# A hybrid state-space block on one core: the first two units of the feed-forward product in turn, and the time-step product of B11 made once

## The chip, the core and the metric

The kernel runs on one core of one Trainium2 chip. The core has five engines with a queue of instructions each: TensorE (PE, matrix products into PSUM banks), VectorE (DVE), ScalarE (ACT), GpSimd (POOL) and SyncE (SP, which here only issues transfers). Each engine takes its instructions strictly in the order of the program's text; an instruction that reads another engine's result waits on a semaphore, and everything behind it on its engine waits with it. The metric is the device time of one execution in microseconds (us), the median of several.

## The reference, cut to what matters

One layer over x (1024 tokens x 1024 features, float32):

```python
h = x + hybrid_mixer(rmsnorm(x, norm_mix_w), w_in, ...)
h = h + swiglu(rmsnorm(h, norm_ffn_w), w_gate, w_up, w_down)
return rmsnorm(h, final_norm_w)

# in hybrid_mixer
u = h @ w_in                               # 1024 x IN_DIM
z, xbc, dt_raw, s_b, s_c, s_x, g_a, g_b = split(u)
dt = softplus(dt_raw + dt_bias)            # 1024 tokens x 32 heads: the "time steps"
...                                        # conv, chunked state-space scan, gated norm, second mixer, w_o

def swiglu(h, w_gate, w_up, w_down):
    return (silu(h @ w_gate) * (h @ w_up)) @ w_down      # hidden size 2816
```

Two places of it are touched: `dt_raw`, which is the normed x times 32 columns of w_in, and the product of the normed h with w_gate and w_up.

## The kernel before, in words

**Products.** The engine's fp32r type holds fewer bits than float32, so every float32 operand is split in two parts of that type: ACT copies the operand (the high part, names ending in h: wh, th), DVE subtracts that copy from the operand (the low part: wl, tl), and three matmuls, high x high (L679), low x high (L680) and high x low (L681), are added up in PSUM. Splitting is `split` (ACT at L76, DVE at L77); one 128x1024 page takes one instruction on each.

**Seven products instead of eight.** Large products are done in a two by two block scheme. Of the turned, normed input, B11 and B21 are the two halves of the features of the first 512 tokens. The second 512 tokens give B12 and B22; of these the kernel keeps B22 and the sums T1 = B12 - B11, T2, T3 and T4 = B21 - T2 with the signs of the scheme. On the weights' side there are A11, A12, A22 and the sums S1 to S4. Product n (1 to 7) multiplies one of each: 1: B11, 2: B21, 3: B22, 4: T4, 5: T1, 6: T2, 7: T3. They run in the order 1, 2, 6, 5, 7, 3, 4.

**The start of the kernel.** Rows of x are loaded, their squares summed (`rows_sq`, ACT at L117 and DVE at L115), scaled (`rows_scale`, L137), turned by PE against the identity (`turn_rows`, L1542, into banks pt), copied out with the norm weight (`turned_out`, ACT at L1549 and DVE at L1551, into br) and split by `put` into th and tl. Then come the first three `Pair`s p0, p1, p2: column blocks of w_in for z, each with a high part (`hi`, ACT at L864), a low part (`lo`, DVE at L868), its matmuls (`pe`, into banks pb and pd) and the copying out (`ev`, ACT at L890). They run product by product: product 1 of p0, p1 and p2, then product 2 of all three, and so on; T1 to T4 are made in between. The text runs: split B11; p0 product 1; `wdt_split` (L1512, splits the 32 columns of w_in for the time steps); `steps_pe(0, 0)`; squares of rows 4 to 7 (L117, L115); p1 high and low part; p1 product 1; squares; copy p0 out (L890); p2 high and low part; p2 product 1; copying out of B21's rows; split B21; scaling of rows 4 to 7; and so on.

**The time steps.** `steps_pe(hf, part)` multiplies the 128x32 weight tiles by the first (hf 0) or second (hf 1) half of the tokens into a bank ts. hf 0 takes B11 (12 matmuls, part 0) and B21 (12, part 1). hf 1 needs B12, which is not kept, and takes B11 and then T1 for it (24 matmuls, part 0), and B22 (12, part 1). Both parts of hf 1 stand just ahead of the first product that uses T3. `time_steps` (at about 113 us) copies both banks out with the bias (L299, ACT, 32x512 each) and does the rest of the softplus and the sums.

**The feed-forward product.** `ffn_phase` (L1163) works on units of 128 columns of w_gate and 128 of w_up for each half of the hidden size. A unit has seven steps, one for each product: split the weights (`prep`, L1241), 24 matmuls (`pe`), copy or add the banks out (`ev`, L1261 and on). Step s = 7u + k is product number k in the order above of unit u. `load_to(n)` issues the weight loads of the first n pages: SP loads a page (L1237), and for S1 to S4 POOL adds a second operand onto it by a transfer that accumulates (L1236, L1239). In text order the steps run 0, 1, 7, 8, 2, 3, 4, 5, 6, 9, 10, ...: products 1 and 2 of the first two units, then what is left of unit 0, then of unit 1. The sums T2, T1, T3, B22 and T4 of this stage are made by a generator, `second_half` (L1191; T4's adds at L1211), which is advanced by one piece behind certain steps. Product n = 7 reads T3, 3 reads B22, 4 reads T4; and steps 4, 5 and 6 are these three of unit 0.

Of the kernel before, what the change touches and what calls it, by code (L numbers as in the profile page):

```python
# [8 lines left out]
F32 = mybir.dt.float32  # L9
F32R = mybir.dt.float32r  # L10
AF = mybir.ActivationFunctionType
ALU = mybir.AluOpType

P = 128
# [6 lines left out]
H = G * HPG  # L21
# [18 lines left out]
def hybrid_block(ctx: ExitStack, tc: tile.TileContext, x, nmw, w_in, cw, cb, dtb, alog, dsk, snw,  # L40
                 wssd, scw, wsc, wo, nfw, wg, wu, wd, fnw, out):
    nc = tc.nc
# [7 lines left out]
    sp = ctx.enter_context(tc.tile_pool(name="sp", bufs=2))  # L50
# [9 lines left out]
    def page(s, shape=(P, 1024), dt=F32):  # L60
        return pp.tile(list(shape), dt, tag="pg", name=nm(s))

    def bank(s):
        return sm.tile([P, 512], F32, tag="sm", name=nm(s))
# [156 lines left out]
    def every(gen):  # L221
        for _ in gen:
            pass
# [24 lines left out]
    dtbc = cp.tile([H, 1], F32, name="dtbc")  # L248
# [38 lines left out]
    pac = cp.tile([P, NT, H], F32, name="pac")  # L287
    V = nc.vector

    def time_steps(ps):  # L290

        a = cp.tile([P, 1], F32, name="a")
        nc.scalar.activation(a, al, AF.Exp)
        V.tensor_scalar_mul(a, a, -1.0)
        t1, t2 = page("ts", (P, 4, 256)), page("ts", (P, 4, 256))
        u, e, r, q, ac = t1[:, 0], t1[:, 1], t1[:, 2], t1[:, 3], t2[:, 0]
        raw = page("tr", (H, S))
        for hf in range(2):
            nc.scalar.activation(raw[:, hf * 512:hf * 512 + 512], ps[hf][:H], AF.Identity, bias=dtbc)  # L299
        for i in range(4):  # L300
            nc.sync.dma_start(u[32 * i:32 * i + 32, :], raw[:, i * 256:i * 256 + 256])
        nc.gpsimd.memset(ac, 1.0)
        nc.gpsimd.memset(ac.rearrange("h (c l) -> h c l", l=P)[:, :, 0:1], 0.0)

        def rest():
            yield
            yield
            yield
            V.scalar_tensor_tensor(e, u, -1.0, u, op0=ALU.mult, op1=ALU.max)
            nc.scalar.activation(e, e, AF.Exp, scale=-1.0)  # L310
            yield
            V.tensor_scalar_add(r, e, 2.0)
            V.reciprocal(r, r)
            yield
            V.tensor_mul(e, e, r)
            V.tensor_mul(q, e, e)
            V.tensor_scalar_mul(r, q, 2.0 / 17)
            yield
            for n in (15, 13, 11, 9, 7, 5, 3):
                V.scalar_tensor_tensor(r, r, 2.0 / n, q, op0=ALU.add, op1=ALU.mult)  # L320
                if n in (11, 5):
                    yield
            V.scalar_tensor_tensor(r, r, 2.0, e, op0=ALU.add, op1=ALU.mult)
            V.scalar_tensor_tensor(u, u, 0.0, r, op0=ALU.max, op1=ALU.add)
            yield
            V.tensor_scalar_mul(e, u, a)
            V.tensor_tensor_scan(q, ac, e, 0.0, op0=ALU.mult, op1=ALU.add)
            yield

            def keep(d, t):  # L330
                for i in range(4):
                    nc.sync.dma_start(d[2 * i:2 * i + 2].rearrange("c h l -> h c l"),
                                      t[32 * i:32 * i + 32, :].rearrange("h (c l) -> h c l", l=P))
            keep(ac_d, q)
            q3 = q.rearrange("h (c l) -> h c l", l=P)
            r3 = r.rearrange("h (c l) -> h c l", l=P)
            V.tensor_sub(r3, q3[:, :, P - 1:P].to_broadcast([P, 2, P]), q3)
            yield
            nc.scalar.activation(r, r, AF.Exp)
            nc.scalar.activation(e, q, AF.Exp)  # L340
            keep(e_d, e)
            yield
            V.tensor_mul(r, r, u)
            yield
            for src, dst in ((u, dtt), (q, pac), (r, wdt)):
                pt = bank("tt")
                for c in range(2):
                    nc.tensor.transpose(pt[:, c * P:(c + 1) * P], src[:, c * P:(c + 1) * P], ident)
                for c in range(2):
                    nc.scalar.activation(dst.rearrange("p (q c) h -> p c q h", c=2)[:, c],  # L350
                                         pt[:, c * P:(c + 1) * P].rearrange("p (q h) -> p q h", h=H), AF.Copy)
            yield
        side.append(rest())
# [324 lines left out]
    def mmc(o, lh, ll, rh, rl, first, last):  # L678
        nc.tensor.matmul(o, lh, rh, start=first, stop=False, skip_group_check=True)  # L679
        nc.tensor.matmul(o, lh, rl, start=False, stop=False, skip_group_check=True)  # L680
        nc.tensor.matmul(o, ll, rh, start=False, stop=last, skip_group_check=True)  # L681
# [147 lines left out]
    def half_b(name, k):  # L829
        h, l = T[name][k // 2]  # L830
        return h[:, k % 2, :], l[:, k % 2, :]
# [331 lines left out]
    def ffn_phase():  # L1163
# [152 lines left out]
        steps = [s for st, _ in units for s in st]  # L1316
# [3 lines left out]
        def load_to(n):  # L1320
            while done[0] < min(n, len(loads)):
                u, f = loads[done[0]]
                units[u][1](f)
                done[0] += 1


        def early_weights():
            load_to(3)
            yield
            load_to(4)  # L1330
            steps[0][0]()
            yield
            steps[1][0]()
            load_to(5)
            yield
            load_to(6)
            yield
            steps[2][0]()
            load_to(8)
            yield  # L1340
            steps[7][0]()
            load_to(9)
            yield

        weights, rows = early_weights(), first_half()
# [10 lines left out]
        gen = second_half(rows1)  # L1356
        steps[0][1]()
        steps[0][2]()
        steps[8][0]()
        steps[3][0]()  # L1360
        steps[1][1]()
        for _ in range(4):
            next(gen, None)
        steps[1][2]()
        for _ in range(4):
            next(gen, None)
        steps[7][1]()
        steps[7][2]()
        next(gen, None)
        steps[8][1]()  # L1370
        next(gen, None)
        steps[8][2]()
        for s in range(2, 6):
            steps[s][1]()
            steps[s][2]()
            next(gen, None)
            if s < 5:
                steps[s + 2][0]()
                load_to(s + 8)
        every(gen)  # L1380

        sq = cp.tile([P, NT, 2], F32, name="sqf")
# [61 lines left out]
                yield  # L1444

        ds = Stream(Gemm(FU, fa_d, fb_d, ORDER, NEG_B, ev_d))
        rest = steps[6:7] + steps[9:]
        rest[1][0]()
        for i, (_, pe, ev) in enumerate(rest):
            load_to(14 + i)  # L1450
            while later and next(later[0], 0) == 0:
                later.pop(0)
            if i >= len(rest) - 4:
                ds.ahead(i - len(rest) + 5, i - len(rest) + 2)
            pe()
            ev()
            if i + 2 < len(rest):
                rest[i + 2][0]()
# [45 lines left out]
    small_loads()  # L1504
    loaded[0] = NF
    steps_ps, wdt_hl = [], []

    def wdt_split():
        for d in range(2):
            t = sp.tile([P, 512], F32R, tag="st", name=nm("wdt"))  # L1510
            wdt_hl.append(t[:, 0:KT * H].rearrange("p (k h) -> p k h", h=H))
        nc.scalar.activation(wdt_hl[0], wdt_s, AF.Copy)  # L1512
        V.tensor_sub(wdt_hl[1], wdt_s, wdt_hl[0].bitcast(F32))

    def steps_pe(hf, part):

        wh, wl = wdt_hl
        if part == 0:
            steps_ps.append(bank("ts"))
        names = ((("B11",), ("B21",)), (("B11", "T1"), ("B22",)))[hf][part]  # L1520
        todo = [(n, k) for n in names for k in range(4)]
        for j, (n, k) in enumerate(todo):
            bh, bl = half_b(n, k)
            kw = 4 * part + k
            mmc(steps_ps[hf][:H], wh[:, kw, :], wl[:, kw, :], bh, bl, j == 0 and part == 0,
                j == len(todo) - 1 and part == 1)

    a0 = rows_sq(xt[0:4], "x", "avav")
    a1 = rows_acc(xt[4:8], "x")
# [95 lines left out]
    gen = second_half()  # L1625
# [25 lines left out]
    for i in range(7 * NF, n_slots):  # L1651
        slot(i)
        if i == 7 * NF + 4:
            time_steps(steps_ps)
            del steps_ps[:]
        if i == 7 * NF + 14:
            d_skip_columns()
        make(i)
        load_pairs((i + 11) // 7 + 1)
        pump()  # L1660
        if i % 3 == 0:
            next(sums, None)
        if i % 3 == 1:
            pump_aux()
        left = n_slots - 1 - i
        if left in (4, 3, 2):
            del T[{4: "T2", 3: "T1", 2: "T3"}[left]]
        if left == 9:
            b12 = [page("br", HB) for _ in range(2)]
            for k in range(2):  # L1670
                nc.sync.dma_start(b12[k], b12_d[k])
        if left == 7:
            direct[0][0].load()
        if left == 4:
            every(put("B12", b12))
        if left == 3:
            direct_hi(direct[0][0])
            direct[1][0].load()
        if left == 2:
            direct_lo(direct[0][0])  # L1680
            pump_scan()
# [42 lines left out]
```

## Time and profile before

| | us |
|---|---|
| median of 3 executions | 1930.08 (1929.77 to 1930.65) |
| profiled execution, its own time | 1931.04 |
| span of its trace (first to last instruction) | 1929.3 |
| PE busy in the span | 1887.9 (98%) |
| DVE busy | 1291.1 (67%) |
| ACT busy | 965.0 (50%) |
| POOL busy | 181.4 (9%) |
| mean granted TensorE clock | 0.995 |

A row of a timeline gives the start in us from the span's beginning, the time to the end of the last of its instructions, the engine, the line, the operation, output<-inputs, partitions x elements, and how many like instructions are drawn together (x1, x2); in square brackets stands how long the engine was idle just ahead of it and what released it. A row of the waits gives the waiting group, what ended the wait, the time waited in total, how many times, and the longest. A row of the windows gives the stretch, its length, and per engine the busy time with the number of instructions; then the granted TensorE clock (1.00 is full speed), the DMA engines' busy share and GB/s.

### The profile page before, as it was taken

The page shows a single profiled execution, that of the slowest core. Times are in us where ns is not written, and L with a number is a line of the kernel's source. Part 1 is how long each engine was busy: PE and PEld are TensorE (multiplying, and loading weights), DVE is VectorE, ACT ScalarE, POOL GpSimd, SP SyncE. Part 2 cuts the span into 40 slices and gives each one's busy share as a digit, 9 for nine tenths or more (in the row PEclk, how much of TensorE's full clock was granted, in tenths as well). Part 3 has the DMA queues.
Part 4 walks back from the last instruction along what each step waited for, and adds up shares of the span by engine and source line. Part 5 has one row for each costly group of instructions (what it writes and reads, how often), then busy time and mean ns, then how long its engine had stood idle before and what let it go on. Part 6 is the DMA issues. An engine that isn't in the chain of part 4 may idle for free.

```text
span 1929.3 us, 24107 instructions
## 1 busy us (share of the span) xinstructions
PE 1887.9 (98%) x8917; PEld 1550.9 (80%) x8917; DVE 1291.1 (67%) x1660; ACT 965.0 (50%) x1533; POOL 181.4 (9%) x168
## 2 busy tenths in 40 slices
PE   7999999999999999999989999999999999999998
PEld 5688888888887888888868888887888888888886
DVE  7667878677774868887878548877444444456465
ACT  5545454444446877777546454465333333345333
POOL 1010111010100101010100000101221121100000
PEclk9999999999999999999989999999999999999999
DMA  5297999988959557768669766736998788867562
GB/s 179 62 260 170 242 233 232 229 207 227 272 138 289 189 180 252 246 220 275 209 243 373 233 222 203 207 125 133 227 205 208 199 192 200 217 259 287 193 196 109
DMA packets 345094, 411.97 MB, mean 214 GB/s; under 512 B 17192, under 2 KB 223744, under 8 KB 344976
## 3 DMA queue, kind: packets, MB, share of 16 engines
q1 hardware_dynamic: 293232, 325.39, 51.7%
q0 software_dynamic: 43680, 55.67, 18.2%
q10 hardware_dynamic: 8064, 29.36, 3.8%
q8 instruction: 70, 1.15, 0.2%
q14 instruction: 48, 0.39, 0.1%
HBM read 320.56 MB, written 143.15 MB: 240 GB/s over the span
## 4 chain that ended last, share of the span: by engine, by line
PE 87%; DVE 6%; ACT 3%; DMA 2%; issue 1%; SPq 0%; ACTq 0%; DVEq 0%
PE pb L679 5%; PE pb L680 5%; PE pb L681 5%; PE gb L680 5%; PE gb L679 5%; PE gb L681 5%; PE fb L681 4%; PE fb L679 4%; PE fb L680 4%; PE pr L81 4%; PE pr L83 4%; PE gd L679 4%; PE gd L680 4%; PE gd L681 4%; PE pr L82 4%; PE pd L679 4%
## 5 line engine op out<-in xcount | busy, mean ns | idle before, releaser
L77 DVE TENSOR_TENSOR wl<-ws,wh 128x1024 fp32r<-128x1024 f32 x77 | 94.0, 1222 | 121.5 <-ACT wh L76 121.5
L680 PE MATMUL gb<-ql,gh 128*128 128x512 f32 x432 | 169.7, 393 | 3.2 <-DVE ql L77 3.2
L679 PE MATMUL gb<-qh,gh 128*128 128x512 f32 x432 | 169.6, 393 | 1.1 <-DVE h L1132 1.1
L681 PE MATMUL gb<-qh,gl 128*128 128x512 f32 x432 | 169.3, 392 | 0.0
L81 PE MATMUL pr<-th,wh 128*128 128x512 f32 x352 | 144.2, 410 | 0.0
L83 PE MATMUL pr<-th,wl 128*128 128x512 f32 x352 | 138.2, 393 | 2.0 <-DVE wl L990 2.0
L681 PE MATMUL fb<-th,wl 128*128 128x512 f32 x352 | 137.2, 390 | 0.8 <-DVE wl L77 0.8
L679 PE MATMUL fb<-th,wh 128*128 128x512 f32 x352 | 137.3, 390 | 0.6 <-ACT wh L76 0.6
L82 PE MATMUL pr<-tl,wh 128*128 128x512 f32 x352 | 137.5, 391 | 0.0
L680 PE MATMUL fb<-tl,wh 128*128 128x512 f32 x352 | 137.1, 390 | 0.0
L679 PE MATMUL gd<-qh,gh 128*128 128x512 f32 x324 | 127.0, 392 | 0.0
L680 PE MATMUL gd<-ql,gh 128*128 128x512 f32 x324 | 126.7, 391 | 0.0
L681 PE MATMUL gd<-qh,gl 128*128 128x512 f32 x324 | 126.7, 391 | 0.0
L77 DVE TENSOR_TENSOR ql<-cb,qh 128x1024 fp32r<-128x1024 f32 x98 | 118.0, 1204 | 2.6 <-ACT qh L76 2.5
L76 ACT ACTIVATE qh<-cb 128x1024 fp32r<-128x1024 f32 x98 | 99.9, 1019 | 38.4 <-PE gb L680 17.2
L679 PE MATMUL fd<-th,wh 128*128 128x512 f32 x264 | 102.8, 390 | 0.0
L681 PE MATMUL fd<-th,wl 128*128 128x512 f32 x264 | 102.8, 390 | 0.0
L680 PE MATMUL fd<-tl,wh 128*128 128x512 f32 x264 | 102.8, 389 | 0.0
L74 DVE SCALAR_TENSOR_TENSOR gl<-ca,gh 128x1024 fp32r<-128x1024 f32 (+1 forms) x60 | 72.8, 1214 | 44.4 <-ACT gh L73 44.4
L680 PEld LDWEIGHTS gb<-ql,gh 128*128 128x128 f32 x432 | 81.8, 189 | 20.7 <-DVE ql L77 3.9
L679 PEld LDWEIGHTS gb<-qh,gh 128*128 128x128 f32 x432 | 81.8, 189 | 18.7 <-DVE h L1132 1.4
L681 PEld LDWEIGHTS gb<-qh,gl 128*128 128x128 f32 x432 | 81.9, 189 | 16.9
(319 smaller groups left out, 4681.7 us busy)
## 6 DMA issues: line engine op xcount, KB each, us to landing
ws<-in_w_in_dram SPq DMA_DIRECT2D x80, 512.0 KB, 7.1
ws<-in_w_gate_dram SPq DMA_DIRECT2D x77, 256.0 KB, 3.9
ws<-in_w_up_dram SPq DMA_DIRECT2D x77, 256.0 KB, 4.4
ca<-u_d SPq DMA_DIRECT2D x35, 512.0 KB, 5.5
ab<-ac_d SPq DMA_DIRECT2D x32, 512.0 KB, 6.9
xbc_g<-cv ACTq DMA_DIRECT2D x24, 512.0 KB, 7.0
ws<-ws POOLq DMA_DIRECT2D x22, 512.0 KB, 6.5
wd_d<-in_w_down_dram SPq DMA_DIRECT2D x20, 512.0 KB, 9.8
```

The source lines that it names most:

```text
L74: nc.vector.scalar_tensor_tensor(lo, src, -1.0, hi.bitcast(F32), op0=ALU.mult, op1=ALU.subtract)
L76: nc.scalar.activation(hi, src, AF.Copy)
L77: nc.vector.tensor_sub(lo, src, hi.bitcast(F32))
L81: nc.tensor.matmul(o, lh, rh, start=first, stop=False)
L82: nc.tensor.matmul(o, lh, rl, start=False, stop=False)
L83: nc.tensor.matmul(o, ll, rh, start=False, stop=last)
L679: nc.tensor.matmul(o, lh, rh, start=first, stop=False, skip_group_check=True)
L680: nc.tensor.matmul(o, lh, rl, start=False, stop=False, skip_group_check=True)
L681: nc.tensor.matmul(o, ll, rh, start=False, stop=last, skip_group_check=True)
```

## The change

Two parts that share nothing but the kernel.

**Time steps.** The 12 matmuls of B11 for the second half of the tokens are dropped. In their place the bank of the first half, which after `steps_pe(0, 0)` holds just B11's part, is copied out with the bias by one ACT instruction (32x512, into a new tile dt11) as soon as that part is done. The second half's bank gets T1 and B22 only, and `time_steps` adds dt11 to it on DVE instead of copying it on ACT.

**Feed-forward product.** After steps 0, 1, 7 and 8 the steps run 2, 9, 3, 10, 4, 11, 5, 6, 12, 13, 14, ...: products 6, 5 and 7 of units 0 and 1 in turn, then 3 and 4 of unit 0 and 3 and 4 of unit 1. The generator of the sums is advanced behind every second of these steps. The weights are loaded ahead in the order of the pages as before, up to page 11 instead of 9 by the early part and further ahead after it; the splitting of step 9's weights now stands behind the eighth piece of the generator, and that of step 3's weights, which stood ahead of step 1's matmuls, now follows step 2.

```diff
@@ time_steps
-    def time_steps(ps):
+    def time_steps(ps, dt11):
...
-        for hf in range(2):
-            nc.scalar.activation(raw[:, hf * 512:hf * 512 + 512], ps[hf][:H], AF.Identity, bias=dtbc)
+        nc.scalar.activation(raw[:, 0:512], ps[0][:H], AF.Identity, bias=dtbc)
+        V.tensor_add(raw[:, 512:1024], dt11, ps[1][:H])
@@ ffn_phase, early_weights
             steps[7][0]()
-            load_to(9)
+            load_to(11)
@@ ffn_phase, the first units
         steps[8][0]()
-        steps[3][0]()
+        seq = [2, 9, 3, 10, 4, 11, 5, 6, 12, 13] + list(range(14, len(steps)))
         steps[1][1]()
         for _ in range(4):
             next(gen, None)
         steps[1][2]()
         for _ in range(4):
             next(gen, None)
+        steps[9][0]()
         steps[7][1]()
         steps[7][2]()
         next(gen, None)
         steps[8][1]()
         next(gen, None)
         steps[8][2]()
-        for s in range(2, 6):
-            steps[s][1]()
-            steps[s][2]()
-            next(gen, None)
-            if s < 5:
-                steps[s + 2][0]()
-                load_to(s + 8)
+        for j in range(6):
+            load_to(12 + j)
+            steps[seq[j]][1]()
+            steps[seq[j]][2]()
+            if j % 2:
+                next(gen, None)
+            steps[seq[j + 2]][0]()
         every(gen)
...
-        rest = steps[6:7] + steps[9:]
-        rest[1][0]()
+        rest = [steps[i] for i in seq[6:]]
         for i, (_, pe, ev) in enumerate(rest):
-            load_to(14 + i)
+            load_to(18 + i)
@@ the start
+    dt11 = sp.tile([P, 512], F32, tag="eb", name="dt11")[:H, :]
...
     def steps_pe(hf, part):
         wh, wl = wdt_hl
         if part == 0:
             steps_ps.append(bank("ts"))
-        names = ((("B11",), ("B21",)), (("B11", "T1"), ("B22",)))[hf][part]
-        todo = [(n, k) for n in names for k in range(4)]
-        for j, (n, k) in enumerate(todo):
-            bh, bl = half_b(n, k)
+        ps = steps_ps[hf][:H]
+        name = (("B11", "B21"), ("T1", "B22"))[hf][part]
+        for k in range(4):
+            bh, bl = half_b(name, k)
             kw = 4 * part + k
-            mmc(steps_ps[hf][:H], wh[:, kw, :], wl[:, kw, :], bh, bl, j == 0 and part == 0,
-                j == len(todo) - 1 and part == 1)
+            mmc(ps, wh[:, kw, :], wl[:, kw, :], bh, bl, k == 0 and part == 0, k == 3)
+        if (hf, part) == (0, 0):
+            nc.scalar.activation(dt11, ps, AF.Identity, bias=dtbc)
@@ second half of the mixer
-            time_steps(steps_ps)
+            time_steps(steps_ps, dt11)
```

What this does to the order of ACT's instructions at the start, where th is B11's high part, wdt the time-step weights, xn the rows whose squares are summed, wh the high part of p1's and then p2's weights, u p0's result and br B21's turned rows. Before:

```order
L76 ACTIVATE th_284<-br_254 128x1024
L76 ACTIVATE th_288<-br_260 128x1024
L1512 ACTIVATE wdt_305<-wdts 128x256
L117 ACTIVATE xn_324,xss_215<-x_90 128x1024
L864 ACTIVATE wh_326<-ws_189 128x1024
L117 ACTIVATE xn_345,xss_215<-x_92 128x1024
L890 ACTIVATE u_347<-pb_292 128x512
L864 ACTIVATE wh_349<-ws_191 128x1024
L1549 ACTIVATE br_366<-pt_264,cols 128x512
```

With the change, the same stretch:

```order
L76 ACTIVATE th_285<-br_255 128x1024
L76 ACTIVATE th_289<-br_261 128x1024
L1513 ACTIVATE wdt_306<-wdts 128x256
L1529 ACTIVATE dt_206<-ts_310,dtbc 32x512
L117 ACTIVATE xn_326,xss_216<-x_90 128x1024
L864 ACTIVATE wh_328<-ws_189 128x1024
L117 ACTIVATE xn_347,xss_216<-x_92 128x1024
L890 ACTIVATE u_349<-pb_293 128x512
L864 ACTIVATE wh_351<-ws_191 128x1024
L1552 ACTIVATE br_368<-pt_265,cols 128x512
```

The copy into dt11, which reads the bank ts, now stands ahead of everything that ACT does for the squares and for the weights of p1 and p2; nothing else of this stretch has moved.

On DVE, around the making of T4 in the feed-forward product (br is T4, made in place from B21 by L1211 and split into tl; L1284 and L1259 are the `ev` of a product 7, L1289 the start of that of a product 3, wl the low part of weights). Before:

```order
L77 TENSOR_TENSOR tl_10896<-br_10718,th_10895 128x1024
L77 TENSOR_TENSOR wl_10900<-ws_10269,wh_10899 128x1024
L1284 TENSOR_TENSOR c_10888<-c_10888,fb_10610 128x512
L1284 TENSOR_TENSOR c_10888<-c_10888,fb_10611 128x512
L1259 TENSOR_TENSOR ub_10700<-c_10888 128x512
L1211 TENSOR_TENSOR br_10516<-br_10516,t_1727_10764 128x1024
L1211 TENSOR_TENSOR br_10529<-br_10529,t_1728_10765 128x1024
L77 TENSOR_TENSOR tl_10938<-br_10516,th_10937 128x1024
L77 TENSOR_TENSOR tl_10942<-br_10529,th_10941 128x1024
L77 TENSOR_TENSOR wl_10946<-ws_10315,wh_10945 128x1024
L1289 TENSOR_TENSOR c_10840<-c_10840,fd_10862 128x512
```

With the change:

```order
L77 TENSOR_TENSOR wl_11008<-ws_10259,wh_11007 128x1024
L1284 TENSOR_TENSOR c_10961<-c_10961,fb_10730 128x512
L1284 TENSOR_TENSOR c_10961<-c_10961,fb_10731 128x512
L1259 TENSOR_TENSOR ub_10810<-c_10961 128x512
L1211 TENSOR_TENSOR br_10515<-br_10515,t_1729_10763 128x1024
L1211 TENSOR_TENSOR br_10528<-br_10528,t_1730_10764 128x1024
L77 TENSOR_TENSOR tl_11047<-br_10515,th_11046 128x1024
L77 TENSOR_TENSOR tl_11051<-br_10528,th_11050 128x1024
L77 TENSOR_TENSOR wl_11055<-ws_10305,wh_11054 128x1024
L1289 TENSOR_TENSOR c_10844<-c_10844,fd_10899 128x512
```

T4 is made behind a product 7 in both; before it is that of unit 0 (step 4), now that of unit 1 (step 11). What stands between the two L1211 and the next product's `ev` is the same.

## The prediction

> **What bounds the kernel now.** I read the page's busy times first.
>
> ```profile
> PE 1887.9 (98%) x8917; PEld 1550.9 (80%) x8917; DVE 1291.1 (67%) x1660; ACT 965.0 (50%) x1533; POOL 181.4 (9%) x168
> ```
>
> PE bounds the run as a whole; work taken from PE is worth its own duration, if PE was the limit where it stood. So the next views are those of the two places: the timelines around the new ACT copy, the waits up to T3, and PE's stalls in the feed-forward product. ACT and then DVE at the start, and PE's matmul that ends `steps_pe(0, 0)`:
>
> ```profile
> 20.16 1.05 ACT L117 ACTIVATE xn<-x 128x1024 f32<-128x1024 f32 x1
> 21.20 1.05 ACT L864 ACTIVATE wh<-ws 128x1024 fp32r<-128x1024 f32 x1
> 23.67 1.05 ACT L864 ACTIVATE wh<-ws 128x1024 fp32r<-128x1024 f32 x1
> 27.09 2.01 ACT L76 ACTIVATE th<-br 128x1024 fp32r<-128x1024 f32 x2 [1.21 <-DVE br L1551]
> ...
> 22.83 1.23 DVE L868 TENSOR_TENSOR wl<-ws,wh 128x1024 fp32r<-128x1024 f32 x1
> 25.11 1.22 DVE L868 TENSOR_TENSOR wl<-ws,wh 128x1024 fp32r<-128x1024 f32 x1
> 31.91 2.08 DVE L137 TENSOR_SCALAR xn<-x,nr 128x1024 f32<-128x1024 f32 x3
> ...
> 25.52 0.39 PE L681 MATMUL ts<-th,wdt 128*32 128x512 f32 x1
> 33.93 1.04 PE L1542 MATMUL pt<-ident,xn 128*128 128x128 f32 x8
> ```
>
> The reader is to see that ACT and DVE run ahead of PE here: ACT is done with the squares and the high parts of p1 and p2 before PE ends the time-step product at 25.52 + 0.39 = 25.91. And that the turned rows on PE (33.93) come just when DVE has scaled them (31.91 + 2.08 = 33.99 for all three): from there PE depends on DVE. The waits from 34 to 76 us, of PE, DVE and ACT, all rows:
>
> ```profile
> PE pt L1542 <- DVE t L1601: 1.1, 3, 0.4
> PE pb L680 <- DVE tl L77: 1.0, 2, 0.8
> PE pb L679 <- ACT th L76: 0.5, 1, 0.5
> PE pd L679 <- DVE t L1601: 0.3, 1, 0.3
> ...
> DVE tl L77 <- ACT th L76: 3.7, 2, 2.1
> DVE t L1601 <- ACT br L1599: 2.6, 2, 1.3
> DVE wl L868 <- ACT wh L864: 1.2, 1, 1.2
> DVE wk L868 <- ACT wk L864: 0.7, 1, 0.7
> ...
> ACT wk L864 <- DVE ws L849: 8.4, 3, 3.2
> ACT wk L864 <- DVE s L847: 5.4, 3, 2.2
> ACT wh L864 <- DVE ws L851: 5.1, 3, 2.8
> ```
>
> No transfer ends a wait here, and neither DVE nor ACT waits for PE. The chain in this stretch is DVE with ACT; PE follows it, being late by a few tenths at a time. So a microsecond lost by DVE at 32 us is still lost at T3.
>
> **The copy into dt11.** It is one ACT instruction, ahead of the squares in ACT's queue, and reads the finished bank: it cannot start before 25.91. The one of its shape in the trace is the copy that it replaces:
>
> ```profile
> L299 ACT ACTIVATE tr<-ts,dtbc x2: 663/664/665, 113.2 to 113.8; 32x512 f32<-32x512 f32 x2
> ```
>
> Two of them start about 0.6 apart, so the squares (L117, before at 20.16) start at about 26.5: 6.3 us late. Behind it are queued squares, p1's high part, squares, p0's copying out, p2's high part, B21's turned rows, B21's split. p1's high part moves from 21.20 to 27.55 and ends at 28.6; p2's, from 23.67 to 30.0, ends at 31.1. DVE takes p1's low part at 28.65 instead of 22.83, the next squares, and p2's low part at 31.1 instead of 25.11: **6.0 us late**, the price of the held queue as DVE sees it (it was waiting for nothing there, so all of it counts). Everything behind keeps its spacing: B21's split, the scaling of rows 4 to 7 (31.91 to 37.9, done at 40.0), the turned rows on PE (33.93 to 40.0). PE's own products of p1 and p2 wait for these low parts too, but are done by about 35, so they are not the limit.
>
> **The dropped matmuls.** T3's split and the time-step product of the second half meet at 75 us:
>
> ```profile
> 73.37 2.20 ACT L76 ACTIVATE th<-br 128x1024 fp32r<-128x1024 f32 x2
> 74.46 2.36 DVE L77 TENSOR_TENSOR tl<-br,th 128x1024 fp32r<-128x1024 f32 x2
> 66.72 0.39 PE L679 MATMUL ts<-th,wdt 128*32 128x512 f32 x1
> 74.84 0.39 PE L681 MATMUL ts<-th,wdt 128*32 128x512 f32 x1
> 75.06 0.39 PE L679 MATMUL pb<-th,wh 128*128 128x512 f32 x1
> 75.74 0.50 PE L680 MATMUL pb<-tl,wh 128*128 128x512 f32 x1 [0.29 <-DVE tl L77]
> ```
>
> The 36 matmuls start from 66.72 to 74.84: 8.12/35 = 0.232 us each, so 12 fewer are 2.78 us less of PE's work. But T3's low part was already late by 0.29 for PE. With everything 6.0 later, its first half ends at 75.68 + 6.0 = 81.7. PE, 6.0 late and 2.78 shorter, ends the time-step product near 78.45, has T3's high part at 80.4, runs one matmul, and waits for the low part until 81.7. The 2.78 us turn into 2.0 + 0.8 us of waiting, and T3's second matmul moves from 75.74 to 81.74. **Net: +6.0 us at T3.** Had the copy not held ACT, the same arithmetic gives nearly nothing: PE would only wait 2.8 us longer for T3. The time-step product was cover, and what it covered is the making of T3.
>
> From 76 us PE is the limit, so what is lost by then stays:
>
> ```profile
> 76.00:100.00 24.00, 24.00 (x107) 19.86 (x107) 15.55 (x18) 12.42 (x14) 0.96 (x1) 1.00 0.42 136
> 965.92:969.33 3.41, 1.28 (x7) 0.72 (x5) 3.41 (x2) 1.73 (x4) 3.32 (x2) 1.00 1.04 408
> 969.33:976.16 6.83, 5.79 (x14) 4.53 (x15) 4.40 (x4) 4.09 (x5) 0.00 (x0) 0.50 0.51 198
> 604.11:607.52 3.41, 2.03 (x13) 1.55 (x12) 0.46 (x1) 1.74 (x2) 0.25 (x1) 1.00 1.07 329
> ...
> 971.39 0.63 PE L679 MATMUL gb<-qh,gh 128*128 128x512 f32 x1
> 971.82 0.63 PE L680 MATMUL gb<-ql,gh 128*128 128x512 f32 x1
> ```
>
> (Window rows: stretch, length, busy PE, PEld, DVE, ACT, POOL, granted clock, DMA share, GB/s.) The first row shows PE full, with DVE at 65% and ACT at 52%. It also hides the change in `time_steps` at 113 us: an ACT copy of 0.66 us goes, a DVE add of about as much comes; if that cover were gone, it would cost at most 0.7.
>
> **The clock behind the new wait.** The other rows show what a wait can do besides. In 965.92 to 969.33 PE was busy for 1.28 of 3.41 us (38%), and for the next 6.83 us the granted clock was 0.50; matmuls then stand 971.82 - 971.39 = 0.43 apart instead of 24.00/107 = 0.224. A stretch that was 60% busy (604.11) kept its clock. The steps of the clock lie on a grid of 3.41 us through 965.92; on it, in this execution, lies 78.46 to 81.87, and my wait leaves PE 0.6 us of work in it (18%). If the grid lies there again, PE runs at half pace for 6.83 us: 6.83 x (1 - 0.224/0.43) = 3.3 us, while no slack is left to hide it. Bounds: 0 (the grid stands so that each stretch keeps over half its work, or PE waits too briefly) to 3.3. I take 3.1, near the upper end, since 18% lies far under the 38% that sufficed; a little of the slow stretch falls in what is left of the wait. The gap that PE gets at 26 to 29.9, waiting for p1's parts, may cost clock too; PE has from 35 to 40 us to make it up.
>
> [...]
>
> **The feed-forward product.** The stalls of this place, on PE at step 6 (product 4 of unit 0), and the two rows that bound the rest:
>
> ```profile
> 1334.86 0.50 PE L679 MATMUL fb<-th,wh 128*128 128x512 f32 x1 [0.59 <-ACT wh L76]
> 1336.37 0.50 PE L681 MATMUL fb<-th,wl 128*128 128x512 f32 x1 [0.78 <-DVE wl L77]
> ...
> 1308.69 4.63 DVE L77 TENSOR_TENSOR tl<-t,th 128x1024 fp32r<-128x1024 f32 x4
> 1312.58 0.39 PE L680 MATMUL fb<-tl,wh 128*128 128x512 f32 x1
> ...
> 1310.63 1.28 POOL L1239 DMA_DIRECT2D ws<-in_w_gate_dram  x1 [59.99 <-DMA ws<-in_w_gate_dram]
> ```
>
> They add up to 0.59 + 0.78 = 1.4 us idle, 1.7 with the slow first matmuls behind them. What is late is T4's split and the high and low parts of step 6's weights, made on DVE in the order shown: product 7's adds, T4's adds, T4's low part, the weights. In the new order T4 is made behind step 11, and between that and step 6 stands step 5 alone, 24 matmuls, the same cover as before. So the stall stays; DVE may come to it up to 0.15 us earlier, since one low part less stands between. Bounds: 0 to -1.7; I take -0.15. Two more things are moved. Step 9's split (ACT 1.05, DVE about 1.15 net) now stands ahead of T2's: T2's first low part is ready at 1309.9 and wanted at 1312.58, so of 2.7 us of room 1.5 are left. And page loads are issued two pages further ahead, four SP issues earlier than before and POOL's accumulating transfers among them; POOL was idle for 60 us ahead of its first one, so these cost nothing unless a page is missing, whose price, by the nearest wait of the kind (a load of some 4 us on the page's list of transfers), would be a few us.
>
> **The sum.** 1930.08 + 6.0 (queue held, net of the dropped matmuls) + 3.1 (half clock) - 0.15 = **1939.0**. Against the profiled execution (1931.04, span 1929.3) the same terms give 1940.0; it lies 0.96 above the median, and I predict the median.
>
> **The rivals.** A change within 0.2% (3.86 us) is what a measurement of this kernel can hardly tell from none: 1926.2 and 1933.9 are the bounds.
> (1) The same loss without half clock: 1930.08 + 6.0 - 0.15 = 1935.9. For it: a grid elsewhere (a boundary in the middle of the gap leaves each stretch about 60% busy, as at 604.11). Against: the 18%.
> (2) The delay at T3 is partly made up between 32 and 76 us, and the kernel ends at about 1933, not told from before: for it, DVE's and ACT's waits for each other are 8 and 19 us, and where both wait, order could give some back; against it, no row shows DVE waiting for anything that is not itself late by 6.0. It needs 2.7 us of 6.0 back.
> (3) Faster: ACT isn't held, or a delay of less than 2.8 us is left at T3, and step 5's cover fills the stall at step 6. The point is 2.8 us at T3: below it the dropped matmuls more than pay. With no delay at all and T3 not waited for, -2.8, and -1.7 in the feed-forward product: 1925.6. Against it: the order of ACT's rows and the 25.91 of PE, and T3's low part being late by 0.29 already.
> (4) The feed-forward order costs: units in turn keep two units' pages, sums and weights alive, and a page or a POOL transfer comes late; 2 to 6 us on top, 1941 to 1945.
> (5) The stall at step 6 is filled, all else as forecast: 1937.4.
>
> **Chances.** Forecast 0.48, (1) 0.24, (2) 0.08, (3) 0.06, (4) 0.10, (5) 0.04. Slower by over 0.2%: 0.48 + 0.24 + 0.10 + 0.04 = 0.86; same 0.08; faster 0.06. The range 1933.5 to 1942.0 holds the forecast, (1), (5), and parts of (2) and (4); the forecast's own is 1937 to 1940.5.
>
> **What would show it.** On ACT the row L1529, dt11<-ts, at about 25.9, ACT idle for over 5 us ahead of it, released by PE ts; L117 behind it at 26.5; DVE's scaling L137 at 37.9; T3's low part at 80.5; PE idle about 2.0 us ahead of T3's first matmul and 0.8 ahead of its second, at 81.7; a granted clock of 0.50 from about 82 to 89 us; behind it the same rows, 9 us late, up to the feed-forward product, and there the same stall of 0.6 and 0.8 us at step 6. Wrong: an ACT row L1529 with less than 3 us of idle ahead, T3's second matmul before 79 us, or new waits of PE past 1300 us.

## The result and the profile after

The changed kernel takes 1936.30 us (median of 7, 1935.22 to 1938.47), against 1930.65 for the kernel before in the same comparison (median of 7, 1929.22 to 1931.55): 5.65 us slower, ratio 1.0031 with a 95% interval of 1.0022 to 1.0040. The profiled execution took 1936.44, its span is 1934.6 against 1929.3. Slower was forecast, 1939.0 with a range of 1933.5 to 1942.0.

The start, ACT, DVE and the last matmul of PE's time-step product in the changed kernel (lines behind the change stand one to three higher than before):

```profile
19.64 0.42 ACT L1513 ACTIVATE wdt<-wdts 128x256 fp32r<-128x256 f32 x1 [1.18 <-DMA wdts<-in_w_in_dram]
25.22 0.68 ACT L1529 ACTIVATE dt<-ts,dtbc 32x512 f32<-32x512 f32 x1 [5.17 <-PE ts L681]
25.81 1.04 ACT L117 ACTIVATE xn<-x 128x1024 f32<-128x1024 f32 x1
26.85 1.04 ACT L864 ACTIVATE wh<-ws 128x1024 fp32r<-128x1024 f32 x1
...
27.92 1.23 DVE L868 TENSOR_TENSOR wl<-ws,wh 128x1024 fp32r<-128x1024 f32 x1 [5.74 <-ACT wh L864]
30.39 1.23 DVE L868 TENSOR_TENSOR wl<-ws,wh 128x1024 fp32r<-128x1024 f32 x1
37.18 2.08 DVE L137 TENSOR_SCALAR xn<-x,nr 128x1024 f32<-128x1024 f32 x3
...
24.80 0.39 PE L681 MATMUL ts<-th,wdt 128*32 128x512 f32 x1
```

ACT stands still for 5.17 us until PE's time-step product ends, then copies, and only then squares. DVE, which waited for nothing here before, waits 5.74 for p1's high part. L137 starts at 37.18 instead of 31.91: 5.27 late, and this execution had come to the time-step product 0.72 sooner than the one before (PE's last matmul of it starts at 24.80, not 25.52), so 6.0 by the held queue. T3, on PE:

```profile
77.33 0.39 PE L681 MATMUL ts<-th,wdt 128*32 128x512 f32 x1
79.75 0.49 PE L679 MATMUL pb<-th,wh 128*128 128x512 f32 x1 [2.04 <-ACT th L76]
81.01 0.79 PE L680 MATMUL pb<-tl,wh 128*128 128x512 f32 x1 [0.77 <-DVE tl L77]
81.60 0.63 PE L681 MATMUL pb<-th,wl 128*128 128x512 f32 x1
82.03 0.63 PE L679 MATMUL pb<-th,wh 128*128 128x512 f32 x1
```

The 12 matmuls fewer are there, and are waited away: 2.04 + 0.77 us, where before it was 0.29. T3's second matmul starts at 81.01 instead of 75.74. The matmuls behind it stand 0.43 apart. The windows (columns as in the prediction):

```profile
77.62:81.03 3.41, 0.61 (x3) 0.21 (x2) 3.36 (x4) 3.06 (x3) 0.00 (x0) 1.00 0.00 0
81.03:84.44 3.41, 3.41 (x8) 2.73 (x9) 1.06 (x1) 0.63 (x1) 0.00 (x0) 0.50 0.00 0
84.44:90.00 5.56, 5.56 (x26) 4.59 (x26) 2.51 (x3) 0.00 (x0) 0.00 (x0) 1.00 0.00 0
```

A stretch with 18% work, and behind it half clock (0.50), for 3.41 us. Much later, in the feed-forward product, step 6 of the changed kernel:

```profile
1356.96 0.50 PE L679 MATMUL fb<-th,wh 128*128 128x512 f32 x1 [0.51 <-ACT wh L76]
1358.41 0.50 PE L681 MATMUL fb<-th,wl 128*128 128x512 f32 x1 [0.72 <-DVE wl L77]
```

The stall that was 0.59 + 0.78 is 0.51 + 0.72: it has moved with its step, not gone.

To see where the time arises, the PE rows of the two traces were put beside each other, matmul by matmul. The start of the same matmul, after minus before:

| place in the trace of before | shift, us | what lies between |
|---|---|---|
| 16.93, 22 us | -0.70, -0.73 | ACT and DVE waited 1.7 and 1.6 us for x at the start of this execution, 2.1 and 2.3 in that of before |
| 34.16 (turned rows) | +5.16 | ACT held |
| 69.48 (last time-step product) | +2.53 | 12 matmuls fewer |
| 75.74 (T3, second matmul) | +5.27 | PE's waits at T3 |
| 95 | +6.84 | half clock |
| 500 | +6.94 | |
| 608 | +5.74 | PE's waits near 600 us, below |
| 1250 | +5.85 | |
| 1370 and on to the end | +5.72 | step 6's stall |

From 22 to 95 us the change costs 7.57 us: 6.0 up to T3 and 1.57 behind it. 1.2 us are given back between 500 and 608 us, where in the kernel before one row stands that the changed one lacks:

```profile
606.58 0.44 PE L426 MATMUL pxt<-ident,x 128*128 128x128 f32 x2 [1.38 <-DMA x<-xbc_g]
```

PE waited there for a load; coming later, it doesn't wait for x. The 1.2 us are a balance: the changed kernel has a wait shortly ahead of it that the kernel before lacks, which by itself raises the shift to 7.99.

```profile
602.48 0.50 PE L679 MATMUL pd<-th,wh 128*128 128x512 f32 x1 [0.70 <-ACT u L897]
```

### The profile page after: what moved, and what is told of

It reads as the page before. It is cut to its first block, busy times and chain, and to the rows that moved or that the text cites. A ratio compares the mean times of both kernels' runs of the same rounds, so it can differ in the third digit from the quotient of the medians.

```text
span 1934.6 us, 24062 instructions
## 1 busy us (share of the span) xinstructions
PE 1889.7 (98%) x8905; PEld 1550.6 (80%) x8905; DVE 1291.5 (67%) x1661; ACT 965.4 (50%) x1533; POOL 181.3 (9%) x168
## 4 chain that ended last, share of the span: by engine, by line
PE 89%; DVE 5%; ACT 3%; DMA 2%; issue 1%; SPq 0%; ACTq 0%; DVEq 0%
PE pb L679 5%; PE pb L680 5%; PE pb L681 5%; PE gb L679 5%; PE gb L680 5%; PE gb L681 5%; PE fb L681 4%; PE fb L679 4%; PE fb L680 4%; PE pr L81 4%; PE gd L679 4%; PE gd L680 4%; PE gd L681 4%; PE pr L83 4%; PE pd L679 4%; PE pd L680 4%
## 5 line engine op out<-in xcount | busy, mean ns | idle before, releaser
L679 PE MATMUL pb<-th,wh 128*128 128x512 f32 x232 | 92.6, 399 | 5.3 <-ACT wh L864 2.8
```

## The experiments

The theory: the copy into dt11 holds ACT's queue, that costs 6.0 us at T3; the dropped matmuls were cover for the making of T3 and are worth nothing there; the gap that they leave lowers the clock; the feed-forward order changes nothing because T4's cover is the same. Each run was compared with the kernel before on the same chip (median 1930.40 for the first four, 1930.41 for the second four). The shifts in the text are those of the same PE rows against the trace of before, as above.

**The copy later.** One row moved, to an idle stretch of ACT at 34 us:

```diff
-        if (hf, part) == (0, 0):
-            nc.scalar.activation(dt11, ps, AF.Identity, bias=dtbc)
...
     p1.ev(1)
     p2.ev(1)
+    nc.scalar.activation(dt11, steps_ps[0][:H], AF.Identity, bias=dtbc)
```

> The changed kernel with one row moved: the copy into dt11 stands behind the copying out of p1's and p2's first products, in an idle stretch of ACT, instead of ahead of the squares. Theory (the held queue costs 6.0 us at T3, and the dropped matmuls are worth nothing there, because T3's split ends no sooner): T3's second matmul is back at about 75.7 us, PE idle 2.8 us more ahead of T3's first two matmuls than in the kernel before, and one window of 3.4 us at half clock behind it (+1.4 us). Time: before + 1.4 - 0.2 = about 1931.9, 4.4 us under the changed kernel. Rival A (once ACT isn't held, the 12 matmuls pay): before - 2.8, about 1927.9. Rival B (the wait of 3.1 us brings no half clock): as before, 1930.5. Rival C (the held queue is not what costs): 1936.

Measured: 1931.4 (11 executions), ratio 1.0006 (0.9997 to 1.0015). That is 4.9 us under the changed kernel's 1936.3, across two comparisons whose kernels before agree within 0.25. T3 on PE, and the window behind it:

```profile
74.80 0.50 PE L679 MATMUL pb<-th,wh 128*128 128x512 f32 x1 [2.04 <-ACT th L76]
76.06 0.53 PE L680 MATMUL pb<-tl,wh 128*128 128x512 f32 x1 [0.76 <-DVE tl L77]
...
72.97:76.38 3.41, 0.82 (x2) 0.48 (x3) 3.36 (x4) 2.76 (x3) 0.00 (x0) 1.00 0.00 0
76.38:79.79 3.41, 3.41 (x9) 2.66 (x8) 0.76 (x1) 0.63 (x1) 0.00 (x0) 0.50 0.00 0
```

T3 is back where it was (76.06 against 75.74, with a start 0.2 to 0.3 later), the same waits of 2.04 and 0.76 stand ahead of it, and half clock follows. The shift against before grows from 0.29 at 22 us to 1.93 at 95: with the queue free, dropping 12 matmuls *costs* 1.6 us in this stretch, the price of the clock alone. Rivals A and C fall by the time and B by the window. The interval holds "no change" as well as the 1.0 us of the medians; it is the rows that show the loss, and they are those of one execution. The eleven executions differ in their mean granted clock, and their times go with it: 1928.99 to 1930.39 at 0.996 (three of them), 1931.05 to 1931.45 at 0.995 (five), 1932.65 to 1933.17 at 0.993 and 0.994 (three). Whether half clock follows T3 in each of them is not shown.

**The feed-forward order alone**, in the kernel before.

> The kernel before with the new order of the feed-forward units alone; the time steps are untouched. Theory: the stall at step 6 (0.6 + 0.8 us) stays, because T4 is still made with one step of cover, so the time is that of before within 0.3 us, about 1930.5. Rival: the order gives 1.5 to 1.8 us, which would be why the changed kernel is 5.7 and not 7.4 us (6.0 + 1.4) slower: about 1929.0. A third: it costs 2 us and more (late pages): 1932.7 or above.

Measured: 1930.5 (11), ratio 0.9999 (0.9990 to 1.0007). The stall at step 6 is there as in the changed kernel:

```profile
1351.05 0.50 PE L679 MATMUL fb<-th,wh 128*128 128x512 f32 x1 [0.51 <-ACT wh L76]
1352.51 0.50 PE L681 MATMUL fb<-th,wl 128*128 128x512 f32 x1 [0.72 <-DVE wl L77]
```

The shift is -0.10 at 1250 us and -0.20 at 1370. The order neither gains nor costs; what the changed kernel gave back did not come from here.

**The matmuls put back.** The early copy holds ACT, but the second half takes B11 and T1 again, 60 matmuls in all, and both banks are copied out by ACT:

```diff
-        name = (("B11", "B21"), ("T1", "B22"))[hf][part]
-        for k in range(4):
+        names = ((("B11",), ("B21",)), (("B11", "T1"), ("B22",)))[hf][part]
+        todo = [(n, k) for n in names for k in range(4)]
+        for j, (n, k) in enumerate(todo):
...
-        V.tensor_add(raw[:, 512:1024], dt11, ps[1][:H])
+        nc.scalar.activation(raw[:, 512:1024], ps[1][:H], AF.Identity, bias=dtbc)
```

> The changed kernel with the 12 matmuls of B11 put back into the second half's time-step product, and the second bank copied out by ACT as before; the early copy into dt11 still holds ACT (its result is not used). PE has 2.8 us more to do than in the changed kernel. Theory (the matmuls were cover for the making of T3, and the gap that they leave brings half clock): PE's waits of 2.0 and 0.8 us at T3 shrink to 0 and 0.3, T3's second matmul stays where it is in the changed kernel (about 81 us), no half clock follows, so the kernel is 1.4 us FASTER than the changed one: about 1934.9. Rival (the matmuls dropped are saved time): 2.8 us slower than the changed kernel, 1939.1. No half clock effect: equal to the changed one, 1936.3.

Measured: 1935.11 (11), ratio 1.0023 (1.0015 to 1.0032). The median is 1.2 us under the changed kernel, with 2.8 us more work on PE. The two intervals overlap, so the times alone don't rank the two kernels; they do exclude the 2.8 us on the other side (1939.1 would be a ratio of 1.0045). The rows decide the rest:

```profile
81.63 0.39 PE L679 MATMUL pb<-th,wh 128*128 128x512 f32 x1
82.30 0.50 PE L680 MATMUL pb<-tl,wh 128*128 128x512 f32 x1 [0.28 <-DVE tl L77]
82.63 0.39 PE L681 MATMUL pb<-th,wl 128*128 128x512 f32 x1
82.86 0.40 PE L679 MATMUL pb<-th,wh 128*128 128x512 f32 x1
```

The wait at T3 is 0.28, as before the change, and the matmuls behind it stand 0.23 apart: no half clock behind T3 (the granted clock is 1.00 from 78 to 90 us). From 22 to 95 us this kernel loses 6.04 us (shift 0.52 to 6.56), which is the held queue by itself. Three terms are thus apart: the hold 6.0, the clock 1.6, and the matmuls 0.

**T3 first.** If T3 is what keeps the dropped matmuls from paying, make it sooner: its product comes ahead of B22's, but B22 was split first.

```diff
-        every(put("B22", raw1[1]))
-        yield
         for k in range(2):
             V.tensor_sub(raw1[0][k], raw1[1][k], raw1[0][k])
         every(put("T3", raw1[0]))
+        yield
+        every(put("B22", raw1[1]))
```

> As the kernel with the late copy, and in the second half of the tokens T3 is made and split ahead of B22's split instead of behind it (T3's product comes ahead of B22's in the order). Theory (what keeps the dropped matmuls from paying is T3 alone): T3's low part is ready some 4 us sooner, PE comes to T3 at about 72.3 without waiting, no half clock: before - 2.8 - 0.3 - 0.2 = about 1927.4. Rival: the wait only moves, to the low parts of p0's to p2's S4 weights or to B22 at product 3, and the time is 1930 to 1932.

Measured: 1934.16 (11), ratio 1.0022 (1.0013 to 1.0030). A miss: 3.8 us slower than before, with neither the 1927.4 nor the rival's 1930 to 1932. Its PE rows:

```profile
75.10 0.64 PE L679 MATMUL ts<-th,wdt 128*32 128x512 f32 x1 [4.84 <-ACT th L76]
76.36 0.64 PE L680 MATMUL ts<-tl,wdt 128*32 128x512 f32 x1 [0.62 <-DVE tl L77]
```

The wait is ahead of ts, not of T3's product: the second half's time-step product reads B22 too (part 1), and stands ahead of T3. The edit moved B22's split behind T3's and left its first reader in front. Half clock follows here too, for 6.83 us; the windows stand further down, under the clock. The waits for B22 should have been traced to every reader, not to product 3 alone.

**T3 first, B22's readers behind it.** The B22 part of the time-step product goes to just ahead of product 3, and B22's split one slot later:

```diff
-    turns = {3: 2, 4: 2, 5: 2, 6: 2, 7: 1, 9: 1, 11: 1, 14: 1}
+    turns = {3: 2, 4: 2, 5: 2, 6: 2, 7: 1, 9: 1, 12: 1, 14: 1}
...
         if i == 4 * NF - 1:
             steps_pe(1, 0)
+        if i == 5 * NF - 1:
             steps_pe(1, 1)
```

> As the kernel with the late copy and T3 ahead of B22, and the second half's B22 part of the time-step product, which stood ahead of T3's product and so waited for B22's split (4.8 us, with 0.6 behind it, in the run before), stands ahead of B22's own product 3, and B22's split one slot later. 48 time-step matmuls as in the changed kernel. Theory (the dropped matmuls pay once PE waits for neither T3 nor B22 there): no PE wait between 60 and 90 us over 0.5, no half clock, 2.8 + 0.3 us less than before at 90 us. Of this some may be lost where PE waits for loads near 606 us (1.4 us in the kernel before, more if PE comes sooner). About 1928, between 1927.3 and 1929. Rival (this stretch has another limit right behind T3): 1930.4 or more.

Measured: 1926.33 (11), ratio 0.9980 (0.9971 to 0.9989): 4.1 us faster than before, ten us faster than the changed kernel, with the same 48 matmuls. That is below the 1927.3 to 1929 forecast. The rows show 3.26 of it from 22 to 95 us (shift 0.48 to -2.78), as forecast; the rest lies within the interval (2.1 to 5.6 us) and is not explained. The whole stretch in one window row:

```profile
60.00:92.00 32.00, 32.00 (x142) 24.46 (x141) 24.96 (x29) 17.70 (x20) 0.00 (x0) 1.00 0.33 89
```

**The same reordering with 60 matmuls.** The kernel before with only T3 first and B22's readers behind it.

> The same reordering (T3 ahead of B22, B22's time-step part ahead of product 3) in the kernel before, with all 60 time-step matmuls and neither the copy into dt11 nor the new order of the feed-forward units. It is the counterpart of the run above: PE is the limit in both, so the 12 matmuls should be worth their 2.8 us between the two, less what the loads near 606 us take back. Theory: before - 0.3, about 1930.1, and 1.5 to 2.8 us over the run above. Rival (the reordering itself is what pays or costs): both alike within 0.5 us.

Measured: 1929.55 (11), ratio 0.9997 (0.9988 to 1.0006). The first matmul of product 3, the time-step product's last part and all of T3's behind it, in the run with 48 matmuls and in this one:

```profile
81.00 0.39 PE L679 MATMUL pd<-th,wh 128*128 128x512 f32 x1
```

```profile
83.50 0.39 PE L679 MATMUL pd<-th,wh 128*128 128x512 f32 x1
```

2.50 apart, with a start that was 0.23 later in the first (shifts of 0.48 and 0.25 at 22 us): 2.73 us for 12 matmuls, where 2.78 was worked out. The medians are 3.2 apart, a little over the 1.5 to 2.8 forecast. In this order, with PE full, the dropped matmuls are worth their time; in the order of the change they were not. The reordering itself takes away the wait of 0.29 at T3 (shift 0.25 to -0.28 from 22 to 95 us) and its time is not told from before.

**T4 one step sooner.** The kernel before, with the feed-forward order of the change, in which the generator's last piece is drawn behind step 4 and the split of step 5's weights:

```diff
-            if j % 2:
+            if j in (1, 3):
                 next(gen, None)
             steps[seq[j + 2]][0]()
+            if j == 4:
+                next(gen, None)
```

> The kernel before with the new order of the feed-forward units, and in it T4 made one step sooner: behind step 4 and the split of step 5's weights, instead of behind step 11. The time steps are untouched. Theory (the stall at step 6, 0.5 + 0.7 us with two slow first matmuls, stays in the changed kernel since T4's cover is one step; with two steps it goes): PE has no wait at step 6, 1.0 to 1.7 us less than with the order alone: about 1929.2. Rival (the work ahead of it on DVE only moves the wait to the weights of step 5 or 6): as the order alone, 1930.5.

Measured: 1928.78 (11), ratio 0.9990 (0.9981 to 0.9999), 1.6 us under before and 1.7 under the order alone. The stretch of the first two units in this kernel, and in the changed one:

```profile
1340.00:1362.00 22.00, 21.97 (x98) 17.82 (x97) 18.29 (x22) 8.91 (x11) 6.08 (x5) 1.00 0.68 145
```

```profile
1340.00:1362.00 22.00, 20.77 (x91) 16.58 (x90) 17.47 (x19) 11.24 (x14) 4.56 (x5) 1.00 0.61 136
```

No PE row of this stretch has a wait any more. T4's adds (L1211) run at 1344.00, ahead of step 11's `ev` (L1284), with a step more of PE's work behind them; the shift falls by 1.57 us between 1250 and 1370.

```profile
1344.00 2.35 DVE L1211 TENSOR_TENSOR br<-br,t 128x1024 f32<-128x1024 f32 x2
1346.41 2.36 DVE L77 TENSOR_TENSOR tl<-br,th 128x1024 fp32r<-128x1024 f32 x2
1348.69 1.28 DVE L1284 TENSOR_TENSOR c<-c,fb 128x512 f32<-128x512 f32 x2
```

So with the units in turn there is room for T4, and the change left it unused, since it drew the generator's last piece one step late. Whether T4 could have been drawn as much sooner in the order of before is not shown: no run has T4 sooner without the units in turn.

**Both repairs.** Late copy, T3 first with B22's readers behind it, and T4 sooner:

> Both repairs together: the late copy, T3 first with B22's parts later, 48 time-step matmuls, the units in turn with T4 made one step sooner. They touch different ends of the run, so their effects should add: about 1926.8 (1925.7 to 1928), under 1930.4 of before by 2.4 to 4.7 us. Rival: no better than the better of the two alone.

Measured: 1924.66 (7), ratio 0.9971 (0.9960 to 0.9982): 5.8 us faster than before and 11.6 faster than the changed kernel, the sum of the two (4.1 + 1.6) within 0.1, and below the 1925.7 to 1928 forecast. In the rows the two are worth 3.3 (shift 0.51 at 22 us to -2.83 at 95) and 1.57 (from -3.69 at 1250 to -5.26 at 1370), 4.9 together; in this execution places that no repair touched, near 600 and 980 us, give another 1.0 (below). This version beats both kernels.

## Why the prediction was right, and where it was off

- **The held queue.** Forecast: the copy starts at 25.9 with over 5 us of idle ahead of it, 6.0 us at DVE, 6.0 at T3. Measured: idle 5.17, at 25.22; 6.0 net of the earlier start, and 6.04 alone in the run with the matmuls put back. Right in place and size. That DVE with ACT sets the pace from 32 to 76 us held in the changed kernel: the +5.16 us at 34.16 stood as +5.27 at T3. The prediction also named the gap that PE gets at 26 us: it may cost clock, and PE can make it up. Both came:

```profile
26.42:29.83 3.41, 1.37 (x5) 0.85 (x6) 1.91 (x2) 3.41 (x7) 0.00 (x0) 1.00 0.00 0
29.83:33.24 3.41, 3.41 (x10) 2.64 (x9) 3.00 (x5) 2.53 (x4) 0.00 (x0) 0.50 0.00 0
39.31 0.87 PE L1545 MATMUL pt<-ident,xn 128*128 128x128 f32 x6 [0.27 <-DVE xn L137]
```

  PE came to the turned rows at 38.67, not by 35 as the prediction had it, and still waited 0.27 for DVE. So this half clock cost nothing, but only 0.27 us of room was left.
- **The dropped matmuls.** Forecast: 2.78 us, waited away as 2.0 + 0.8. Measured: 2.04 + 0.77; worth 2.73 us where PE waits for nothing, and nothing here. Right. The prediction also said that with the copy out of the way the same arithmetic gives nearly nothing; the late copy gave -1.6 us in the stretch. It had not carried the clock into that sentence.
- **The clock.** This is the step that failed in size: 3.1 us at half clock, measured 1.57 from T3's second matmul to 95 us (1.3 over the seven intervals from 81.60 to 84.53, the rest just ahead of them). Half clock came behind the wait as forecast (0.50 from 81.03 us), at 0.43 us from matmul to matmul. The duration was taken from one row, 6.83 us, which holds two windows:

```profile
969.33:972.74 3.41, 2.37 (x6) 1.89 (x7) 3.41 (x4) 2.89 (x3) 0.00 (x0) 0.50 0.63 242
972.74:976.16 3.42, 3.42 (x10) 2.65 (x9) 0.99 (x1) 1.19 (x2) 0.00 (x0) 0.50 0.40 154
```

  In the first PE was still waiting (busy for 2.37 of 3.41 us) and the clock of the next was still 0.50; behind the second, full one it was 1.00 again, from 976.16. Behind T3 the first slow window was full at once (3.41 of 3.41), and the clock was 1.00 behind it, from 84.44. Cut in two, the row would have shown a slow window that was not full. The run with T3 first has the other case behind its wait of 4.84 us, a slow window with little work and then a nearly full one:

```profile
69.35:72.76 3.41, 0.91 (x4) 0.22 (x2) 2.23 (x3) 1.54 (x2) 0.00 (x0) 1.00 0.00 0
72.76:76.18 3.42, 0.64 (x1) 0.13 (x1) 1.29 (x2) 2.95 (x3) 0.00 (x0) 0.50 0.00 0
76.18:79.59 3.41, 3.23 (x8) 1.38 (x9) 1.26 (x2) 0.63 (x1) 0.00 (x0) 0.50 0.00 0
```

  That nearly a whole window lay in the wait was partly luck. The prediction carried the grid of one execution over to another and put the window at 78.46 to 81.87; it lay at 77.62 to 81.03.

  Of the windows shown, those with 0.61 of 3.41 us of work (18%, the changed kernel), 0.82 (24%, late copy), 0.91 (27%, T3 first), 1.28 (38%, the row at 965.92) and 1.37 (40%, the row at 26.42) were each followed by half clock. Behind the one at 604.11, with 2.03 us (60%), the clock stayed at 1.00.
- **The feed-forward product.** Forecast -0.15, measured -0.13 in the changed kernel's trace and -0.10 in that of the order alone. Right.
- **What was missing:** the 1.2 us given back near 600 us. From 76 us on the prediction took PE as the limit up to the end. It named DMA waits only at the feed-forward stage. Its own row at 604.11, shown there for the clock, was only 60% busy. Between 590 and 618 us the shift changes by 0.0 (T4 sooner, T3 first), -1.2 (the changed kernel) and up to -3.1 (matmuls put back), and runs that came sooner than before show it too (-2.3 in the reordering with 60 matmuls, -2.4 with both repairs). So it is not only slack for the delayed: the reordering with 60 matmuls comes to this place 0.33 sooner than before and does not wait for x at all, where the kernel before waited 1.38 us and the one with the late copy 0.3. The load of x was issued at 595.28 us in the kernel before and at 602.10 in the changed one. PE's waits there for ACT (L897: 0.70 us in the changed kernel, none in that before) and DVE (L990: none and 1.5) differ as well. A second such place lies between 965 and 1000 us, where the shift changes by -0.4 (matmuls put back) to +1.4 (both repairs). How much of a delay of 6 us this takes back on the average is left open; no run was made for it. The sum of the terms as measured, 6.0 + 1.6 - 0.1 = 7.5, stands against 5.65 measured between medians (4.2 to 7.7 by the interval).

The time came out near that of rival (1), 1935.9 without half clock, but not for its reason: half clock was there, shorter, and the stretch near 600 us took back about as much as it cost. That near match is luck. (The sum of rival (5) is 1937.5, not 1937.4.) Rival (3), faster, became true of the kernel with its copy moved and T3's cover replaced: it needed both. Rivals (2), (4) and (5) find no support: the delay was not made up before 76 us, no page came late, and the stall at step 6 stayed.

## What to carry to other kernels

Before an instruction that reads a late result is put into an in-order queue, read what stands behind it there: a copy of 0.68 us cost 6.0, because three splits and two squares stood behind it, and 9 us later in the same queue, where ACT was idle, it was free (T3 at 76.06 us, before 75.74). Work taken off the busiest engine paid here only where nothing it waits for was hidden by that work (the 12 matmuls: 2.73 us in one order, nothing in the other); look at the wait just behind the place (0.29 us at T3 was the sign), and move what is waited for, with all its readers, by as much as is taken away. When an order makes room, the work that the room is for must be drawn into it.

## What the hardware showed that was not expected

The clock's windows did not lie at the same place, counted from the start of the span, in the executions profiled: half clock began at 81.03 us in the changed kernel and at 76.38 in that with the late copy, and the two don't lie on one grid of 3.41 us (they are 4.65 apart). The grid of the kernel before, on which the prediction put a boundary at 81.87, is a third. In both runs most of one window happened to fall into the wait; what a boundary in the middle of it would do was not seen. By an estimate from these rows, 2.81 us of waiting split evenly over two windows of 3.41 leaves each 59% of work, about the 60% of the row at 604.11, behind which the clock stayed at 1.00; what would follow here is not shown. And in these two runs a wait of 2.0 + 0.8 us with a matmul of 0.5 between cost about 1.6 us more behind it, over half of the wait again.
